# Four 4 KB places for raw weights in place of two of 8 KB, and loads and splits in pieces of at most 1024 elements

## The chip, the cores and the metric

The kernel runs on one core of a Trainium2 chip. The metric is device time in microseconds (us) for one execution; lower is better. The core's engines are TensorE (PE, with its weight loads as PEld), VectorE (DVE), ScalarE (ACT), GpSimd (POOL) and SyncE (SP). SP computes nothing here: it issues nearly all transfers, in the order of its queue.

## The reference

Two transformer blocks over 512 tokens of width 1024, in float32.

```python
def first_block(x, ...):
    h = rmsnorm(x, norm_mix)
    proj = h @ w_in                       # queries, keys, values, gates of two attentions
    y_a = swa_sink_attention(qa, ka, va)  # 8 heads, window 128
    k_cmp = compress(kc, cmp_w1_k, ...)   # gelu(blocks @ w1) @ w2; v_cmp the same
    y_b = nsa_attention(qb, k_cmp, v_cmp, ksl, vsl, kw, vw, gates)
    merged = sigmoid(g_a) * (y_a @ w_up_a) + sigmoid(g_b) * (y_b @ w_up_b)
    x = x + merged @ w_out
    ug = causal_dwconv(rmsnorm(x, norm_ffn) @ w_ffn_in, conv_w, conv_b)
    u, g = split(ug)                      # 2816 each
    x = x + (silu(g) * u) @ w_ffn_out
    return rmsnorm(x, norm_final)

def second_block(x, mem, ...):            # MLA, differential and memory attention
    proj = rms_norm(x) @ w_in_2
    y = concatenate([y_mla, y_diff, y_mem]) * silu(z)
    return x + y @ w_out_2
```

## The kernel before

Every product of activations and weights is done as three matmuls on rounded halves (`mm3`, lines 302 to 309): each operand is H (its value rounded to the matmul type) plus L (the rest), and the three are wH·xH, wH·xL and wL·xH.

So each block of weights goes through three steps. `wload` (line 125) has SP load it from HBM into a tile `raw`. `wsplit` (line 135) writes `wH` on ACT (line 139) and `wL = raw - wH` on DVE or POOL (line 140); each of wH and wL has three buffers of 4 KB of a partition. Then PE reads both. All raw tiles share one tag with two buffers ("places"), each as large as the largest tile: 8 KB of a partition, or 2048 float32 elements. A load can be issued only when the earlier tile in its place has been read for the last time, by the subtraction of line 140.

`dense_steps` (line 314) goes over output columns in tiles of 128. It loads a chunk of 256 columns (8 blocks of 128 rows, so 2048 elements, 1 MB) at a time and splits one tile of 128 columns (1024 elements) per step; a tile is 24 matmuls of 512 columns. Where only 128 columns are wanted (the keys, the compress inputs), the load has 1024 elements, and takes one of the two places all the same. With one group of rows, the next tile's split (and, at a new chunk, its load) is called two k before the end of a tile (`WA`). `ffn` uses it for `w_ffn_in` (a chunk for u, then one for g, 11 column tiles in each of two halves `hf`; the eleventh tile is alone, 128 wide) and for `w_ffn_out` (two groups of 6 and 5 row blocks, 1536 and 1280 elements). `up` has a chunk of 512 with four row blocks. `nat_steps` (line 1124) is the product with tokens on the partitions. `values` loads 4 x 416 elements, and `compress` 8 x 256 of `w1`, used in two halves. `fetch` (line 221) brings weights of the second block, split ahead of time (`presplit`) and stored as H and L, back: three of five into wH and wL, two of five as one tile of 8 KB in the tag `raw`.

The stages follow one another in one program: the norm; the products for the window attention; then `pipeline` over its 8 heads, with `fill1` woven in (memory keys, keys, `compress`, and the queries `qg` of the second attention); then the second attention with `fill2` (the gate product `ga` and `up`); `gb`, `up`, `w_out`; the FFN; and the second block. A scheduler of the framework lays out the program: for each engine it sets one order from the order of the code and its own estimates, and each engine then runs its queue strictly in that order. An instruction that waits holds all that is queued behind it on its engine. The waits for buffers are put in by the framework.

Of the kernel before, what the change touches and what calls it, by code (L numbers as in the profile page):

```python
# [85 lines left out]
class Build:  # L86
# [36 lines left out]


    def wload(self, src, ktn, w):
        raw = self.wp.tile([128, ktn, w], F32, tag="raw", name="raw", bufs=2)
        if isinstance(src, (list, tuple)):
            n = 128 // len(src)
            for i, s in enumerate(src):
                self.nc.sync.dma_start(raw[i * n:(i + 1) * n], s)  # L130
        else:
            self.nc.sync.dma_start(raw, src)
        return raw

    def wsplit(self, raw):
        ktn, w = raw.shape[1], raw.shape[2]
        H = self.wp.tile([128, ktn, w], F32R, tag="wH", name="wH", bufs=3)
        L = self.wp.tile([128, ktn, w], F32R, tag="wL", name="wL", bufs=3)
        self.nc.scalar.activation(H, raw, AF.Copy)  # L139
        self.leng.tensor_sub(L, raw, f32(H))  # L140
        return H, L
# [79 lines left out]
    def fetch(self, key):  # L221

        dst, n, w = self.held.pop(key)
        self.turn = getattr(self, "turn", -1) + 1
        if self.turn % 5 < 3:
            T = [self.wp.tile([128, n * w], F32R, tag=t, name=t, bufs=3) for t in ("wH", "wL")]
            for i in range(2):
                self.nc.sync.dma_start(f32(T[i]), f32(dst[:, i]))
        else:
            t = self.wp.tile([128, 2, n * w], F32R, tag="raw", name="wHL", bufs=2)  # L230
            self.nc.sync.dma_start(f32(t), f32(dst))
            T = [t[:, i] for i in range(2)]
        return [t.rearrange("p (k c) -> p k c", k=n) for t in T]

# [79 lines left out]
    def dense_steps(self, src, groups, c0, cw, xH, xL, evac, chunk=256, tag="mm", mt=128, pre=None):  # L314
# [5 lines left out]
        def weights(i, gi):  # L320
            if pre is not None:
                return next(pre)
            c, o = tiles[i]
            w = min(chunk, c0 + cw - c)
            if o == 0 and gi == 0:
                raws[c] = [self.wload(src(k0, k1, c, w), k1 - k0, w) for k0, k1 in groups]
            return self.wsplit(raws[c][gi][:, :, o:o + min(mt, w - o)])
        k_last = groups[-1][1] - 1
# [177 lines left out]
    def block1(self):  # L506
# [45 lines left out]
        def values():  # L552
            pv = [self.psum(t) for t in ("O", "O", "mm", "mm")]
            for kk in range(0, 8, 4):
                raw = self.wp.tile([128, 4, 416], F32, tag="raw", name="raw", bufs=2)
                for o, c0, w in ((0, 640, 128), (128, 1664, 128), (256, 1920, 160)):
                    nc.sync.dma_start(raw[:, :, o:o + w], W(kk, kk + 4, c0, w))
                for k2 in range(0, 4, 2):
                    H, L = self.wsplit(raw[:, k2:k2 + 2])
                    for b in range(4):  # L560
                        tb = slice(128 * b, 128 * b + 128)
                        for i in range(2):
                            k = kk + k2 + i
                            self.mm3(pv[b][:, :408], hH[:, k, tb], hL[:, k, tb], H[:, i, :408], L[:, i, :408],
                                     k == 0, k == 7)
            for b in range(4):
                self.split(pv[b][:, :384].rearrange("p (h d) -> p h d", d=64), V2[:, b, :, :64], V2[:, b, :, 64:])
                nc.scalar.activation(gate[:, b], pv[b][:, 384:408], AF.Tanh, scale=0.5)
            nc.vector.tensor_scalar(gate, gate, 0.5, 0.5, op0=ALU.mult, op1=ALU.add)
# [166 lines left out]
        QB = []  # L736
        qg = self.dense_steps(W, K8, 768, 512, HH, HL, qevac(QB))

        def fill1():
# [28 lines left out]
            def compress(i):  # L768
# [5 lines left out]
                for k0 in (0, 4, 8, 12, None):  # L774
                    if k0 is not None:
                        if k0 % 8 == 0:
                            raw = self.wload(w1[:, k0:k0 + 8], 8, 256)
                        le = self.leng
                        self.leng = nc.gpsimd if CE >> (k0 // 4) & 1 else nc.vector
                        parts.append((k0, *self.wsplit(raw[:, k0 % 8:k0 % 8 + 4])))  # L780
                        self.leng = le
# [189 lines left out]
        def up(W, y, evac):  # L971
            W = W.rearrange("(g k p) c -> g p k c", g=2, p=64)
            return self.dense_steps(lambda k0, k1, c, w: [W[g][:, k0:k1, c:c + w] for g in range(2)], [(0, 4)], 0, D,
                                    [y[k][:, 0] for k in range(4)], [y[k][:, 1] for k in range(4)], evac, chunk=512)

# [148 lines left out]
    def nat_steps(self, src, ktn, cols, xH, xL, evac, nb=4, tags=("mm", "S"), t=0, tail=False, kf=0, pre=None):  # L1124


        for i, pieces in enumerate(cols):
# [12 lines left out]
            held = []  # L1140
            kr = ktn - kf if pre is not None or (ktn - kf) * w <= 2048 else (ktn - kf) // 2
            step = min(kr, max(1, 1024 // w))
            for k0 in [b + i for b in range(kf, ktn, kr) for i in range(0, kr, step)]:
                k1 = min(ktn, k0 + step)
                if pre is None and (k0 - kf) % kr == 0:
                    raw = self.wp.tile([128, kr, w], F32, tag="raw", name="raw", bufs=2)
                    o = 0
# [826 lines left out]
```

## Time before, and its profile

| | |
|---|---|
| Median of 3 runs | 1069.96 us (1069.77 to 1073.72) |
| The profiled execution's own time | 1068.34 us |
| Its span | 1066.4 us |
| Granted TensorE clock over the span | 0.996 |
| Instructions | 15435 |
| HBM read / written | 128.83 MB / 39.08 MB |

The span reaches from the first to the last instruction of the profiled execution; the rest of that execution's time lies around it. In rows of a timeline the first column is the start in us, the second the duration in us (from the first start to the last end where several are merged), then engine and line, and in brackets how long the engine sat idle before it and what ended that. A matmul's recorded duration overlaps with the next one's, so its rate is read from starts or counts.

### The profile page before, as it was taken

What the parts mean: (1) busy time and instruction counts of PE and PEld (TensorE: products, weight loads), DVE (VectorE), ACT (ScalarE), POOL (GpSimd) and SP (SyncE); (2) the same over time, 40 slices, a digit from 0 to 9 for tenths busy, and PEclk for the clock granted to TensorE, in tenths of its full rate; (3) what the DMA queues carried; (4) which work ended last, traced back from release to release, by engine and by line L of the source; (5) the groups of instructions that cost most, each with busy time, mean ns of one, the idle gap of its engine ahead of it and who ended that gap; (6) DMA issues with size and microseconds to landing.
All of it is one profiled execution on the core that took longest, in us unless ns stands there. A gap on an engine that the chain in (4) does not pass through costs nothing.

```text
span 1066.4 us, 15435 instructions
## 1 busy us (share of the span) xinstructions
PE 1027.0 (96%) x5425; PEld 866.1 (81%) x5425; DVE 751.1 (70%) x1603; ACT 581.3 (55%) x1127; POOL 230.7 (22%) x361
## 2 busy tenths in 40 slices
PE   5999898989999999999999999999999999999898
PEld 4897777878878888888888888887889997887798
DVE  6669884487882375678985478988633497989982
ACT  6557764577783244345553445555643545977630
POOL 4323124222321048000000200000350128230200
PEclk9999999999999999999999999999999999999999
DMA  6645436221213363255769978868855662266442
GB/s 190 177 110 173 104 85 155 52 45 35 57 49 84 79 180 99 80 157 156 224 207 313 313 242 239 255 218 270 296 192 168 220 216 82 80 198 198 138 159 80
DMA packets 131341, 169.98 MB, mean 159 GB/s; under 512 B 8548, under 2 KB 101450, under 8 KB 130112
## 3 DMA queue, kind: packets, MB, share of 16 engines
q1 hardware_dynamic: 127904, 161.50, 49.0%
q0 software_dynamic: 3360, 7.49, 2.9%
q8 instruction: 43, 0.70, 0.3%
q14 instruction: 34, 0.28, 0.1%
HBM read 128.83 MB, written 39.08 MB: 157 GB/s over the span
## 4 chain that ended last, share of the span: by engine, by line
PE 75%; DVE 13%; ACT 4%; DMA 4%; issue 3%; SPq 0%; POOL 0%; POOLq 0%; ACTq 0%; DVEq 0%
PE ps_mm L304 19%; PE ps_mm L309 19%; PE ps_mm L308 19%; PE ps_S L1366 3%; PE ps_T L498 3%; DMA raw<-in_w_in 2%; DVE wL L140 2%; PE ps_O L1395 1%; PE ps_O L1397 1%; PE ps_S L309 1%; PE ps_S L308 1%; PE ps_S L304 1%; DVE PTL L112 1%; ACT e L489 1%; DVE e L487 1%
## 5 line engine op out<-in xcount | busy, mean ns | idle before, releaser
L139 ACT ACTIVATE wH<-raw 128x1024 fp32r<-128x1024 f32 (+4 forms) x145 | 137.3, 947 | 192.1 <-PE ps_mm L308 148.4
L140 DVE TENSOR_TENSOR wL<-raw,wH 128x1024 fp32r<-128x1024 f32 (+4 forms) x130 | 146.3, 1127 | 90.9 <-ACT wH L139 90.5
L304 PE MATMUL ps_mm<-nH,wH 128*128 128x512 f32 x416 | 162.7, 391 | 0.6 <-DVE qL L118 0.6
L309 PE MATMUL ps_mm<-nH,wL 128*128 128x512 f32 x416 | 162.5, 391 | 0.0
L308 PE MATMUL ps_mm<-nL,wH 128*128 128x512 f32 x416 | 162.5, 391 | 0.0
L489 ACT ACTIVATE e<-e,mn 128x256 f32<-128x256 f32 (+5 forms) x160 | 86.3, 541 | 26.8 <-DVE mn L487 25.5
L304 PE MATMUL ps_mm<-hH,wH 128*128 128x512 f32 x232 | 93.6, 404 | 0.0
L309 PE MATMUL ps_mm<-hH,wL 128*128 128x512 f32 x232 | 91.7, 395 | 0.0
L304 PEld LDWEIGHTS ps_mm<-nH,wH 128*128 128x128 f32 x416 | 78.2, 188 | 16.5 <-DVE qL L118 0.8
L308 PE MATMUL ps_mm<-hL,wH 128*128 128x512 f32 x232 | 91.3, 393 | 0.0
L309 PEld LDWEIGHTS ps_mm<-nH,wL 128*128 128x128 f32 x416 | 78.1, 188 | 15.8
L308 PEld LDWEIGHTS ps_mm<-nL,wH 128*128 128x128 f32 x416 | 78.2, 188 | 15.5
L111 ACT ACTIVATE PTH<-ps_T 128x512 fp32r<-128x512 f32 (+1 forms) x108 | 55.6, 528 | 31.6 <-PE ps_T L498 30.9
L112 DVE TENSOR_TENSOR PTL<-ps_T,PTH 128x512 fp32r<-128x512 f32 (+1 forms) x108 | 63.7, 606 | 10.6 <-ACT PTH L111 9.5
L304 PE MATMUL ps_mm<-aH,wH 128*128 128x512 f32 x176 | 68.5, 390 | 1.6 <-ACT aH L111 1.5
L308 PE MATMUL ps_mm<-aL,wH 128*128 128x512 f32 x176 | 68.5, 389 | 0.0
L309 PE MATMUL ps_mm<-aH,wL 128*128 128x512 f32 x176 | 68.5, 389 | 0.0
L498 PE MATMUL ps_T<-ident,e 128*128 128x128 f32 x368 | 62.6, 277 | 6.1 <-DVE e L1739 3.6
L498 PEld LDWEIGHTS ps_T<-ident,e 128*128 128x128 f32 x368 | 44.7, 141 | 22.2 <-DVE e L1739 4.4
L1080 POOL MEMSET cv<- 128x2 f32 x44 | 4.3, 100 | 235.5 <-DVE cc L1084 229.1
L309 PEld LDWEIGHTS ps_mm<-hH,wL 128*128 128x128 f32 x232 | 43.8, 189 | 9.0 <-DVE wL L140 0.2
L304 PEld LDWEIGHTS ps_mm<-hH,wH 128*128 128x128 f32 x232 | 43.8, 189 | 7.2 <-ACT wH L139 0.8
(584 smaller groups left out, 2596.5 us busy)
## 6 DMA issues: line engine op xcount, KB each, us to landing
raw<-in_w_ffn_in SPq DMA_DIRECT2D x20, 1024.0 KB, 5.8
raw<-in_w_in SPq DMA_DIRECT2D x12, 1024.0 KB, 7.6
pre<-in_w_in SPq DMA_DIRECT2D x17, 512.0 KB, 5.6
raw<-in_w_ffn_out SPq DMA_DIRECT2D x8, 768.0 KB, 5.7
raw<-in_w_ffn_out SPq DMA_DIRECT2D x8, 640.0 KB, 6.2
xt<-in_x SPq DMA_DIRECT2D x8, 512.0 KB, 5.0
raw<-in_w_out SPq DMA_DIRECT2D x4, 1024.0 KB, 5.3
pre_z<-preH SPq DMA_DIRECT2D x16, 256.0 KB, 5.1
```

Source lines behind the costliest of these rows:

```text
L111: nc.scalar.activation(H, src, AF.Copy)
L112: nc.vector.tensor_sub(L, src, f32(H))
L139: self.nc.scalar.activation(H, raw, AF.Copy)
L140: self.leng.tensor_sub(L, raw, f32(H))
L304: ins = mm(ps, wH, xH, start=first, stop=False)
L308: mm(ps, wH, xL, start=False, stop=False)
L309: mm(ps, wL, xH, start=False, stop=last)
L487: nc.vector.tensor_tensor_reduce(e, ps, bias, op0=ALU.add, op1=ALU.min, scale=1.0, scalar=3e38, accum_out=mn)
L489: nc.scalar.activation(e, e, AF.Exp, scale=-1.0, bias=mn, accum_out=sm)
L498: nc.tensor.transpose(ps[:, 128 * i:128 * i + 128], blk, self.ident)
L1366: nc.tensor.matmul(ps[:, :n], q[:, 128 * b:128 * b + 128], k[:, :n], start=i == 0, stop=i == len(prods) - 1)
L1395: mm(out, v2(kb), H[:, c], start=first, stop=False)
```

## The change

Raw tiles now hold at most 1024 elements of a partition (4 KB), and there are four of them. `wload` cuts a load along the row blocks into equal pieces of at most 1024 elements, a transfer and a place for each; `wsplit` takes one or several pieces and writes each part of `wH` and `wL` with an instruction of its own. The H and L of a fetched 8 KB tile become two tiles of 4 KB with a transfer each. `qg` loads chunks of 128 columns in place of 256, `up` chunks of 256 in place of 512, `compress` and `values` load per split, and `nat_steps` loads at most 1024 elements at a time.

```diff
+    def rawtile(self, *shape):
+        return self.wp.tile([128, *shape], F32, tag="raw", name="raw", bufs=4)
+
     def wload(self, src, ktn, w):
-        raw = self.wp.tile([128, ktn, w], F32, tag="raw", name="raw", bufs=2)
...
+        n = -(-ktn * w // 1024)
+        step = -(-ktn // n)
+        out = []
+        for k0 in range(0, ktn, step):
+            k1 = min(ktn, k0 + step)
+            raw = self.rawtile(k1 - k0, w)
+            v = src(k0, k1)
...
+                self.nc.sync.dma_start(raw, v)
+            out.append((k0, raw))
+        return out
+
+    def wsplit(self, *pieces):
...
-        self.nc.scalar.activation(H, raw, AF.Copy)
-        self.leng.tensor_sub(L, raw, f32(H))
+        k = 0
+        for p in pieces:
+            c = slice(k, k + p.shape[1])
+            k += p.shape[1]
+            self.nc.scalar.activation(H[:, c], p, AF.Copy)
+            self.leng.tensor_sub(L[:, c], p, f32(H[:, c]))
         return H, L
...
-            t = self.wp.tile([128, 2, n * w], F32R, tag="raw", name="wHL", bufs=2)
-            self.nc.sync.dma_start(f32(t), f32(dst))
-            T = [t[:, i] for i in range(2)]
+            T = [self.wp.tile([128, n * w], F32R, tag="raw", name="wHL", bufs=4) for _ in range(2)]
+            for i in range(2):
+                self.nc.sync.dma_start(f32(T[i]), f32(dst[:, i]))
...
-                raws[c] = [self.wload(src(k0, k1, c, w), k1 - k0, w) for k0, k1 in groups]
-            return self.wsplit(raws[c][gi][:, :, o:o + min(mt, w - o)])
+                raws[c] = [self.wload(lambda a, b: src(k0 + a, k0 + b, c, w), k1 - k0, w) for k0, k1 in groups]
+            return self.wsplit(*(r[:, :, o:o + min(mt, w - o)] for _, r in raws[c][gi]))
...
-            for kk in range(0, 8, 4):
-                raw = self.wp.tile([128, 4, 416], F32, tag="raw", name="raw", bufs=2)
+            for kk in range(0, 8, 2):
+                raw = self.rawtile(2, 416)
...
-        qg = self.dense_steps(W, K8, 768, 512, HH, HL, qevac(QB))
+        qg = self.dense_steps(W, K8, 768, 512, HH, HL, qevac(QB), chunk=128)
...
-                        if k0 % 8 == 0:
-                            raw = self.wload(w1[:, k0:k0 + 8], 8, 256)
+                        raw = self.rawtile(4, 256)
+                        nc.sync.dma_start(raw, w1[:, k0:k0 + 4])
...
-                                    [y[k][:, 0] for k in range(4)], [y[k][:, 1] for k in range(4)], evac, chunk=512)
+                                    [y[k][:, 0] for k in range(4)], [y[k][:, 1] for k in range(4)], evac)
...
-            kr = ktn - kf if pre is not None or (ktn - kf) * w <= 2048 else (ktn - kf) // 2
+            kr = ktn - kf if pre is not None or (ktn - kf) * w <= 1024 else (ktn - kf) // 2
```

## Rows read from the trace of the kernel before

**Rows 1.** The page: busy time and share of each engine; the chain by engine.
```profile
PE 1027.0 (96%) x5425; PEld 866.1 (81%) x5425; DVE 751.1 (70%) x1603; ACT 581.3 (55%) x1127; POOL 230.7 (22%) x361
...
PE 75%; DVE 13%; ACT 4%; DMA 4%; issue 3%; SPq 0%; POOL 0%; POOLq 0%; ACTq 0%; DVEq 0%
```

**Rows 2.** Timeline of PE: starts that followed idle time, with their releasers.
```profile
127.92 0.39 PE L699 MATMUL ps_O<-PTH,V 128*128 128x256 f32 x1 [2.11 <-ACT PTH L111]
...
149.64 0.38 PE L699 MATMUL ps_O<-PTH,V 128*128 128x256 f32 x1 [0.82 <-ACT PTH L111]
150.37 0.39 PE L700 MATMUL ps_O<-PTL,V 128*128 128x256 f32 x1 [0.34 <-DVE PTL L112]
...
171.85 1.14 PE L834 MATMUL ps_T<-w2v,hv 128*128 128x64 f32 x8 [2.31 <-POOL hv L827]
...
741.86 0.50 PE L304 MATMUL ps_mm<-aH,wH 128*128 128x512 f32 x1 [1.47 <-ACT aH L111]
```

**Rows 3.** Timeline of ACT: splits of raw tiles that waited for a transfer.
```profile
125.94 1.06 ACT L139 ACTIVATE wH<-raw 128x1024 fp32r<-128x1024 f32 x1 [2.15 <-DMA raw<-in_w_in]
...
146.73 1.06 ACT L139 ACTIVATE wH<-raw 128x1024 fp32r<-128x1024 f32 x1 [3.46 <-DMA raw<-in_w_in]
...
168.08 1.06 ACT L139 ACTIVATE wH<-raw 128x1024 fp32r<-128x1024 f32 x1 [5.04 <-DMA raw<-in_w_in]
...
723.63 0.85 ACT L139 ACTIVATE wH<-raw 128x768 fp32r<-128x768 f32 x1 [2.46 <-DMA raw<-in_w_ffn_out]
```

**Rows 4.** The chain in order of time, 100 to 176 us: start, us, what.
```profile
107.88 1.14 DVE wL L140
...
116.52 1.20 DVE wL L140
...
117.73 8.13 DMA raw<-in_w_in
...
127.03 1.23 DVE wL L140
...
136.94 1.73 DVE wL L140
...
138.72 7.90 DMA raw<-in_w_in
...
156.58 1.24 DVE wL L140
...
157.83 10.16 DMA raw<-in_w_in
```

**Rows 5.** Windows: us, busy of each engine, clock, DMA share, GB/s.
```profile
100.00:150.00 50.00, 44.59 (x252) 36.15 (x250) 44.15 (x98) 34.49 (x72) 14.39 (x12) 1.00 0.41 95
...
550.00:600.00 50.00, 49.89 (x221) 40.98 (x220) 29.29 (x42) 19.70 (x31) 0.20 (x2) 1.00 0.90 301
...
700.00:750.00 50.00, 48.53 (x215) 39.71 (x214) 42.24 (x62) 28.73 (x44) 0.40 (x4) 1.00 0.75 243
```

**Rows 6.** Timeline of DVE in the FFN, a half block, a weight split, the next.
```profile
712.52 0.68 DVE L207 TENSOR_TENSOR preL<-pre,preH 128x512 fp32r<-128x512 f32 x1
713.12 1.22 DVE L140 TENSOR_TENSOR wL<-raw,wH 128x1024 fp32r<-128x1024 f32 x1
714.25 0.74 DVE L1083 SCALAR_TENSOR_TENSOR cc<-cv,vec_norm_ffn,cc 128x512 f32<-128x512 f32 x1
```

**Rows 7.** Timeline of SP: the first loads of `w_ffn_out` in the second half.
```profile
716.32 3.08 SPq L132 DMA_DIRECT2D raw<-in_w_ffn_out x2
```

**Rows 8.** The tile `raw`: instructions by line, ns min/median/max, forms.
```profile
L139 ACT ACTIVATE wH<-raw x145: 613/1058/1075, 12.6 to 783.7; 128x1024 fp32r<-128x1024 f32 x93, 128x512 fp32r<-128x512 f32 x16, 128x768 fp32r<-128x768 f32 x16, 128x640 fp32r<-128x640 f32 x16
L140 DVE TENSOR_TENSOR wL<-raw,wH x130: 683/1221/1983, 23.6 to 784.5; 128x1024 fp32r<-128x1024 f32 x86, 128x768 fp32r<-128x768 f32 x16, 128x640 fp32r<-128x640 f32 x16, 128x512 fp32r<-128x512 f32 x8
```

**Rows 9.** DMA issues: count, KB each, median us from issue to landing.
```profile
raw<-in_w_ffn_in SPq DMA_DIRECT2D x20, 1024.0 KB, 5.8
...
raw<-in_w_ffn_in SPq DMA_DIRECT2D x4, 512.0 KB, 4.9
```

More of the change, by code (lines that the diff above doesn't have):

```diff
@@ L122, in show @@
             self.nc.sync.dma_start(self.dbg[name], ap)
+    def rawtile(self, *shape):
+        return self.wp.tile([128, *shape], F32, tag="raw", name="raw", bufs=4)
     def wload(self, src, ktn, w):
-        raw = self.wp.tile([128, ktn, w], F32, tag="raw", name="raw", bufs=2)
[L127 to L136, printed above, removed]
+        n = -(-ktn * w // 1024)
[5 more added lines that the diff above has]
+            v = src(k0, k1)
+            if isinstance(v, (list, tuple)):
+                m = 128 // len(v)
+                for i, t in enumerate(v):
+                    self.nc.sync.dma_start(raw[i * m:(i + 1) * m], t)
+            else:
+                self.nc.sync.dma_start(raw, v)
+            out.append((k0, raw))
+        return out
+    def wsplit(self, *pieces):
+        w = pieces[0].shape[2]
+        ktn = sum(p.shape[1] for p in pieces)
         H = self.wp.tile([128, ktn, w], F32R, tag="wH", name="wH", bufs=3)
         L = self.wp.tile([128, ktn, w], F32R, tag="wL", name="wL", bufs=3)
-        self.nc.scalar.activation(H, raw, AF.Copy)
-        self.leng.tensor_sub(L, raw, f32(H))
+        k = 0
[4 more added lines that the diff above has]
+            self.leng.tensor_sub(L[:, c], p, f32(H[:, c]))
         return H, L
@@ L553, in values @@
             pv = [self.psum(t) for t in ("O", "O", "mm", "mm")]
-            for kk in range(0, 8, 4):
-                raw = self.wp.tile([128, 4, 416], F32, tag="raw", name="raw", bufs=2)
+            for kk in range(0, 8, 2):
+                raw = self.rawtile(2, 416)
                 for o, c0, w in ((0, 640, 128), (128, 1664, 128), (256, 1920, 160)):
[L557 to L565, printed above, removed]
+                    nc.sync.dma_start(raw[:, :, o:o + w], W(kk, kk + 2, c0, w))
+                H, L = self.wsplit(raw)
+                for b in range(4):
+                    tb = slice(128 * b, 128 * b + 128)
+                    for i in range(2):
+                        k = kk + i
+                        self.mm3(pv[b][:, :408], hH[:, k, tb], hL[:, k, tb], H[:, i, :408], L[:, i, :408],
+                                 k == 0, k == 7)
             for b in range(4):
@@ L775, in compress @@
                     if k0 is not None:
-                        if k0 % 8 == 0:
-                            raw = self.wload(w1[:, k0:k0 + 8], 8, 256)
+                        raw = self.rawtile(4, 256)
+                        nc.sync.dma_start(raw, w1[:, k0:k0 + 4])
                         le = self.leng
                         self.leng = nc.gpsimd if CE >> (k0 // 4) & 1 else nc.vector
-                        parts.append((k0, *self.wsplit(raw[:, k0 % 8:k0 % 8 + 4])))
+                        parts.append((k0, *self.wsplit(raw)))
                         self.leng = le
@@ L1145, in nat_steps @@
                 if pre is None and (k0 - kf) % kr == 0:
-                    raw = self.wp.tile([128, kr, w], F32, tag="raw", name="raw", bufs=2)
+                    raw = self.rawtile(kr, w)
                     o = 0
```

## The prediction

> **What bounds the kernel now.** I read the page first: PE is busy for 1027.0 of 1066.4 us and 75% of the chain that ended last is PE's [rows 1]. So only what leaves PE idle (39.4 us in all) or makes the idle time longer can move the end; a faster load that no one waits for is worth nothing. Next, the windows: in the FFN PE never pauses (221 matmuls in 49.89 us, so 0.226 us each, at full clock) although DMA is at its most loaded there, 0.90 of its time, while the window attention with its woven products keeps PE at 44.59 of 50 us [rows 5]. Then I went through PE's timeline for every start behind idle time. Some lie ahead of the first product and touch no raw weight; many short ones belong to the softmax work. Five are left that I trace back to a weight split: 2.11, 0.82, 0.34, 2.31 and 1.47 us [rows 2], 7.05 in all. That is nearly the whole of what the change can win.
>
> How a load stops PE although PE waits for no weight: ACT runs its queue in order, and four splits on it sat 2.15, 3.46, 5.04 and 2.46 us for a transfer [rows 3]. Behind the first stands PTH, for which PE then waited until 127.92; behind the second the PTH of 149.64, and its L part on DVE. Behind the third, DVE's subtraction is late, behind it on DVE the copy `hid`, POOL's `hv` after that, and PE starts again at 171.85 [rows 2].
>
> And why the transfers are late: the chain shows each as issued when a place comes free and not before. A subtraction starts at 116.52 and takes 1.20 us; the load is issued at 117.73. One starts at 136.94 and takes 1.73; the next load goes at 138.72. One starts at 156.58 and takes 1.24; the third goes at 157.83 [rows 4]. They then need 8.13, 7.90 and 10.16 us to land. In this stretch a 512 KB tile of keys holds an 8 KB place, so two loads are all that can be on their way or in use.
>
> **The change part by part.**
>
> *Four places in the window attention.* Write down the order of loads there: second compress weight quarter w1k1, w1k2, w1k3, the v input (1408), q0, q1, w1v0, w1v1, q2, w1v2, w1v3, q3, then the two pieces of the gate chunk ga. Each now takes one place of four, so a load waits for the split of the item four before it.
> - q0 waits for w1k1, whose subtraction begins at 107.88 and takes 1.14 [rows 4]: issue from 109.02 in place of 117.73, 8.71 us sooner. ACT came to that split 2.15 us before 125.94 [rows 3], at 123.79; even at 8.13 us the load lands by 117.2. The wait and the 2.11 us of PE go.
> - q2 waits for q0, whose subtraction ends at 127.03 + 1.23 = 128.26 [rows 4]: 10.46 us sooner than 138.72. At 7.90 it lands at 136.2, and ACT came at 146.73 - 3.46 = 143.27 [rows 3]. The 0.82 and 0.34 us go.
> - ga's first piece waits for q2, which was split at 146.73 [rows 3], so it goes some 8 us sooner than 157.83; its second waits for w1v2, split somewhere between there and 157.82 [rows 4], and may still hold ACT. Of the 2.31 us I count 1.6 as gained, between 0 and all.
> That is 2.11 + 0.82 + 0.34 + 1.6 = 4.9 us. Who is late next is DVE: it is busy for 44.15 of 50 us there [rows 5], so up to half of this may come back as waits for DVE: 2.4 to 5.6 us (with the 2.31 whole).
>
> *The end of the FFN's second half.* The eleventh column tile of u and of g is a 512 KB load each, and the two fill both places, so the loads of `w_ffn_out` go at 716.32 and after [rows 7], right behind the subtraction that starts at 713.12 [rows 6] and SP's stores. The split waits 2.46 us [rows 3], DVE loses time behind it, and PE waits 1.47 us at 741.86 for aH [rows 2]. With four places the two single tiles take two and the first two pieces of `w_ffn_out` the others, which come free with the chunk before, a tile of 24 matmuls (24 x 0.226 = 5.4 us) sooner. The wait of 2.46 goes. I take 1.0 of the 1.47, as DVE stays full (42.24 of 50 [rows 5]); bounds 0 and 1.47.
>
> *More instructions.* Of the 93 splits with 1024 elements [rows 8], 68 become two by the code (window queries 4, ga 8, gb 8, `w_out` 8, `w_ffn_in` 40); all 32 with 768 or 640 do too. So 100 more activations and 100 more subtractions. On a full DVE the step from start to start is 713.12 - 712.52 = 0.60 us for 512 elements and 714.25 - 713.12 = 1.13 for 1024 [rows 6]: two halves cost 1.20, so 0.07 more each, 7 us over the kernel if all were on DVE (93 - 86 = 7 splits of that size have it on POOL [rows 8]). By recorded durations the upper bound is 2 x 0.683 - 1.221 = 0.145 on DVE and 2 x 0.613 - 1.058 = 0.168 on ACT [rows 8], 15 and 17 us. None of it is in the stretch of 112 to 172, where every split keeps its size. In the FFN it lies beside 5.4 us of matmuls per tile with DVE at 84% [rows 5]; at 0.07 to 0.15 per tile the cover holds. What would be late without the cover is aH and aL at the end of a half: some four doubled subtractions stand there, 0.3 us, which I count as lost. Against it, the first half of a split can feed matmuls before the second is done; PE in the FFN has no pause that this could fill, so nothing.
>
> *More transfers.* A chunk of 1 MB becomes two loads of 512 KB; packets stay as long in HBM (1 KB rows) but for qg (512 B). By the rows, 512 KB of `w_ffn_in` land in 4.9 us and 1 MB in 5.8 [rows 9]. A chunk lasts PE 2 x 5.4 = 10.8 us, so even two loads one after the other (9.8) fit. Cost nothing; the other end of the bound is a rival below. The Trainium skill speaks against smaller loads: "DMA: Bandwidth & Descriptors", Rules for kernel authors, wants at least 1 MiB per DMA, and its fit under "Anatomy of one DMA" is 2.0 us plus the bytes over 436 GB/s; by that fit, an estimate, two halves in a row take 6.4 us where one whole takes 4.4. The trace is slower than the fit but has the same shape, and either result is below what a chunk lasts PE, so by the page too the sum stays.
>
> *The fetched weights, `up`, `values`, `compress`, `nat_steps`.* The same bytes are held and the same number of tiles is in use; H and L take a place each. SP issues more, which only matters where SP is late, and PE shows no wait on a transfer there. Nothing, within 1 us either way, as the scheduler will lay out all queues anew.
>
> **Sum.** -4.9 - 1.0 + 0.3 = -5.6 us against the profiled execution's 1068.34: 1062.7. The median stands 1.62 us above that execution, so 1064.4, or 0.52% less than 1069.96.
>
> **The rivals.**
> - *DVE takes over.* The transfers come early, but DVE, already at 44.15 of 50 [rows 5], sets the pace in the stretch, so that half of the 4.9 and none of the 1.0 is won and the 0.3 lost: -2.15, or 1067.8. For it: DVE is 13% of the chain [rows 1]. Against: while ACT waited, DVE waited too.
> - *The loads don't come earlier.* The places are there, but SP's order puts each load just ahead of its split, and all ACT waits stay: 1070, the time of before with at most the 0.3. Against it: three times out of three the load left within 0.05 us of the subtraction that freed its place [rows 4], so SP stood ready.
> - *Slower: halves land one after the other.* If in the FFN each 512 KB piece took as long as 1 MB now (5.8 us [rows 9]), a chunk would need 11.6 us against 10.8, and each of 20 two-tile chunks would add 0.8 us: 16 us, with the rest as forecast about 1080. It decides from 5.4 us a piece. For it: DMA at 0.90 [rows 5]. Against: the bytes and packets of the FFN stay the same, and pieces can overlap.
> - *More than counted.* All 7.05 us go, and with them some 3 of PE's other idle time (39.4 in all), as splits off ACT's and DVE's way let the softmax work come sooner: 1060.
>
> **How the numbers follow.** Forecast (1061 to 1066.5) 0.45; DVE takes over 0.20; loads no earlier 0.12; slower 0.08; more 0.15. The predicted time is 1064.4. The range 1058 to 1070.5 leaves out the slower case and a little at either end. Half a percent, 5.35 us, is about what a measurement of this kernel tells from no change; below 1064.6 it is faster. Of the forecast's span of 5.5 us, 3.6 lie below that, two thirds, which makes 0.29; with the last case 0.44 faster. The slower case is 0.08, and the rest, 0.48, no change.
>
> **What would show it.** Right: ACT's splits in the window attention no longer wait for DMA, and PE's pauses of 2.11, 0.82 and 2.31 are gone; the stretch up to the gate product is 4 to 5 us shorter; the pause before the first aH product of `w_ffn_out` shrinks; in the FFN PE stays at 221 or 222 matmuls per 50 us. Wrong: loads still leave behind the subtraction two before; new waits of PE for DVE in 112 to 172; in the FFN, splits that wait for transfers with PE pausing; or a new order of the queues that opens pauses far from the weights.

## The result, and the profile after

The changed kernel takes 1058.75 us (median of 4 runs, 1058.01 to 1060.0), against 1070.1 for the kernel before beside it (1069.77 to 1073.72): a ratio of 0.9879, 95% interval 0.986 to 0.9898. That is 11.35 us less, where 5.6 were forecast. The direction was right and most of the places were, and the time lies in the range, but the size is out by a factor of two. The profiled execution has a span of 1056.3 us and took 1058.04.

The page after, its lines on busy time and on the chain by engine [rows 1]:

```profile
PE 1022.2 (97%) x5425; PEld 863.8 (82%) x5425; DVE 759.5 (72%) x1697; ACT 591.1 (56%) x1227; POOL 226.1 (21%) x367
...
PE 79%; DVE 13%; ACT 4%; issue 2%; DMA 1%; POOLq 0%; POOL 0%; SPq 0%; ACTq 0%; DVEq 0%
```

The span lost 10.1 us. PE's idle time fell only from 39.4 to 34.1 us; the other 4.8 came out of its *busy* time, with the same 5425 matmuls. Half of the gain was never idle time in the records, so a sum of pauses could not have found it. At a lower clock a matmul is busy for longer, as below, and behind a pause one is recorded as longer too: the two with PTH in [rows 2] take 0.39 and 0.38 us, most of that form with no pause ahead 0.28. What else lies in the 4.8 us stays open.

Where it went: windows that end at the same matmul in both kernels. First the kernel before, from 95 us on (us, then busy time and count of PE, PEld, DVE, ACT and POOL; PE's granted clock; DMA share; GB/s):

```profile
95.00:125.40 30.40, 28.73 (x165) 23.38 (x164) 27.91 (x59) 22.02 (x47) 8.64 (x12) 1.00 0.48 113
125.40:148.20 22.80, 19.89 (x117) 16.61 (x116) 19.65 (x49) 14.33 (x29) 4.49 (x2) 1.00 0.33 73
148.20:172.80 24.60, 20.04 (x105) 15.41 (x103) 17.51 (x30) 15.06 (x28) 5.02 (x8) 1.00 0.48 122
172.80:213.00 40.20, 40.20 (x202) 33.76 (x202) 15.55 (x47) 21.09 (x46) 17.08 (x14) 1.00 0.37 89
213.00:226.30 13.30, 11.10 (x55) 9.34 (x54) 12.17 (x33) 7.14 (x18) 3.43 (x3) 0.87 0.35 79
```

And the changed kernel in the same five stretches, then in the three of [rows 5]:

```profile
95.60:124.60 29.00, 27.88 (x165) 23.11 (x164) 27.38 (x60) 24.54 (x51) 8.56 (x12) 1.00 0.53 128
124.60:145.30 20.70, 20.07 (x118) 16.91 (x118) 19.67 (x50) 14.70 (x34) 6.71 (x3) 1.00 0.32 88
145.30:165.50 20.20, 18.66 (x105) 15.45 (x103) 16.63 (x30) 13.02 (x24) 5.06 (x9) 1.00 0.60 155
165.50:205.70 40.20, 40.20 (x202) 33.72 (x202) 14.79 (x46) 20.72 (x49) 15.91 (x18) 1.00 0.27 63
205.70:217.50 11.80, 9.85 (x55) 7.81 (x54) 11.59 (x33) 6.67 (x17) 3.57 (x4) 1.00 0.44 90
...
100.00:150.00 50.00, 48.17 (x280) 40.09 (x279) 47.07 (x109) 40.25 (x83) 15.05 (x12) 1.00 0.47 115
550.00:600.00 50.00, 49.72 (x219) 40.62 (x218) 26.63 (x48) 20.43 (x40) 3.16 (x10) 1.00 0.92 290
700.00:750.00 50.00, 49.88 (x220) 40.93 (x220) 41.39 (x65) 29.09 (x52) 4.41 (x6) 1.00 0.77 255
```

Stretch by stretch the change is worth -1.4, -2.1, -4.4, 0 and -1.5 us. The third is the one to look at: 105 matmuls in both, PE idle 4.56 before and 1.54 after (-3.0), and their busy time down by 1.4 as well, at a full clock in both. A further 1.3 us went behind these stretches, nearly all at the end of the FFN, and the first 95 us cost 0.6; together that is the 10.1. The first and the last of the five stretches, 2.9 us, are in no term of the sum. The FFN's steady part is as it was: the window has 219 matmuls, at a DMA share of 0.92, where 221 or 222 were forecast, but matmul for matmul (the k-th of one kernel against the k-th of the other) nothing moves: from the 2750th to the 3400th both take 147.3 us.

The loads leave sooner, as forecast. SP issues those for q0, q2 and the gate product's first piece at these times (starts, changed kernel), against 117.73, 138.72 and 157.83 before [rows 4]; 8.71, 10.46 and some 8 us were forecast, 9.8, 17.0 and 13.9 came (up to 3 us of it is the kernel's own lead by then):

```profile
107.93 0.38 SPq L143 DMA_DIRECT2D raw<-in_w_in  x1
...
121.69 0.37 SPq L143 DMA_DIRECT2D raw<-in_w_in  x1
...
143.93 0.37 SPq L143 DMA_DIRECT2D raw<-in_w_in  x1
```

They also land sooner (median us from issue to landing, kernel before, then the changed one):

```profile
raw<-in_w_in SPq DMA_DIRECT2D x12, 1024.0 KB, 7.6
...
raw<-in_w_in SPq DMA_DIRECT2D x29, 512.0 KB, 4.6
```

Why the middle is shorter is seen on ACT. Its waits for raw weights by source (us in all, times, longest), kernel before:

```profile
ACT wH L139 <- DMA raw<-in_w_ffn_out: 12.7, 5, 3.9
ACT wH L139 <- DMA raw<-in_w_in: 10.6, 3, 5.0
ACT wH L139 <- DMA raw<-in_w_ffn_in: 3.4, 1, 3.4
```

The changed kernel:

```profile
ACT wH L157 <- DMA raw<-in_w_ffn_out: 15.9, 6, 3.6
ACT wH L157 <- DMA raw<-in_w_ffn_in: 8.1, 5, 3.8
ACT wH L157 <- DMA raw<-in_w_mem_kv: 2.1, 1, 2.1
```

The three waits for `in_w_in` [rows 3] are gone. In the FFN ACT now waits longer than before, and PE hardly notices: it has one new pause there, of 0.28 us at 551.25, for an aH at the end of the first half. PE's pauses of 0.25 us or more between 110 and 172 us are now these (timeline, starts behind idle time); none goes back to a transfer, the largest is DVE's:

```profile
112.04 0.39 PE L716 MATMUL ps_O<-PTH,V 128*128 128x256 f32 x1 [0.58 <-ACT PTH L111]
117.39 0.51 PE L322 MATMUL ps_mm<-hH,wH 128*128 128x512 f32 x1 [0.27 <-ACT wH L157]
133.11 0.30 PE L825 MATMUL ps_T<-ident,gx 62*128 62x62 f32 x2 [0.58 <-DVE gx L821]
...
157.69 0.39 PE L717 MATMUL ps_O<-PTL,V 128*128 128x256 f32 x1 [1.24 <-DVE PTL L112]
```

Ahead of that PTL in DVE's queue stands a weight subtraction that is recorded as 1.77 us beside two GpSimd instructions; one of the same size takes 0.67 at 154.00:

```profile
154.94 1.77 DVE L158 TENSOR_TENSOR wL<-raw,wH 128x512 fp32r<-128x512 f32 x1
```

### The profile page after: what moved, and what is told of

It is laid out like the page before. It is cut to its first block, busy times and chain, and to the rows that moved or that the text cites. A ratio compares the mean times of both kernels' runs of the same rounds, so it can differ in the third digit from the quotient of the medians.

```text
span 1056.3 us, 15851 instructions
## 1 busy us (share of the span) xinstructions
PE 1022.2 (97%) x5425; PEld 863.8 (82%) x5425; DVE 759.5 (72%) x1697; ACT 591.1 (56%) x1227; POOL 226.1 (21%) x367
## 4 chain that ended last, share of the span: by engine, by line
PE 79%; DVE 13%; ACT 4%; issue 2%; DMA 1%; POOLq 0%; POOL 0%; SPq 0%; ACTq 0%; DVEq 0%
PE ps_mm L322 20%; PE ps_mm L327 20%; PE ps_mm L326 20%; PE ps_S L1383 3%; PE ps_T L516 2%; DVE wL L158 2%; DVE e L505 1%; DVE PTL L112 1%; PE ps_O L1414 1%; PE ps_O L1412 1%; PE ps_S L327 1%; PE ps_S L326 1%; PE ps_S L322 1%; ACT e L507 1%; DMA xt<-in_x 1%
## 5 line engine op out<-in xcount | busy, mean ns | idle before, releaser
L157 ACT ACTIVATE wH<-raw 128x512 fp32r<-128x512 f32 (+4 forms) x245 | 150.0, 638 | 196.4 <-PE ps_mm L326 134.6
L158 DVE TENSOR_TENSOR wL<-raw,wH 128x512 fp32r<-128x512 f32 (+3 forms) x224 | 161.9, 741 | 85.9 <-ACT wH L157 82.9
L505 DVE CUSTOM_DVE_ANT_0 e<-ps_S,G 128x128 f32<-128x128 f32 (+1 forms) x64 | 30.7, 485 | 27.3 <-PE ps_S L1383 27.1
```

The lines of the kernel that those rows point to most:

```text
L157: self.nc.scalar.activation(H[:, c], p, AF.Copy)
L158: self.leng.tensor_sub(L[:, c], p, f32(H[:, c]))
L505: nc.vector.tensor_tensor_reduce(e, ps, bias, op0=ALU.add, op1=ALU.min, scale=1.0, scalar=3e38, accum_out=mn)
```

## The experiments

The theory after this reading had three parts: (a) splits in the window attention and at the end of the FFN no longer hold ACT for a transfer; (b) GpSimd's queue has one long subtraction in a better place, so that VectorE isn't held up beside it; (c) with fewer pauses PE's clock falls less often. The rivals were that pieces alone, or places alone, hold the gain. Each run stands against runs of the kernel before on the same chip (medians 1070.6 to 1071.8), so ratios compare best; that of the changed kernel is 0.9879.

**Pieces without places.** The kernel before, its two places of 8 KB loaded and split in pieces of at most 1024 elements. The chunks stay as they were, so the queries' loads still bring 256 columns:

```diff
-            self.nc.sync.dma_start(raw, src)
...
+            for k0 in range(0, ktn, step):
+                k1 = min(ktn, k0 + step)
+                self.nc.sync.dma_start(raw[:, k0:k1], src[:, k0:k1])
...
+            c = slice(k0, min(ktn, k0 + step))
+            self.nc.scalar.activation(H[:, c], raw[:, c], AF.Copy)
+            self.leng.tensor_sub(L[:, c], raw[:, c], f32(H[:, c]))
```

> The kernel before with loads and splits cut into the same pieces of at most 1024 elements, but the two places of 8 KB kept. Theory (places): the gain is that a small load no longer blocks 8 KB, so here the window attention keeps its pauses; ACT's splits wait for transfers of w_in again, some 10 us in all, and the time is 1068 to 1072. Rival (pieces): shorter instructions and loads feed PE sooner, so most of the gain is here too, 1058 to 1063.

Measured 1067.52, ratio 0.9959 (0.9938 to 0.9979), just under the theory's range. But that is a gain and a loss. By 205 us it is 3.9 us ahead of the kernel before, matmul for matmul; at the ends of the two halves of the FFN it loses 3.8 and 2.1. PE waits there (its timeline):

```profile
556.54 0.73 PE L312 MATMUL ps_mm<-aH,wH 128*128 128x512 f32 x2 [2.13 <-ACT aH L111]
...
740.66 0.50 PE L312 MATMUL ps_mm<-aH,wH 128*128 128x512 f32 x1 [2.04 <-ACT aH L111]
```

and windows just behind them show the granted clock at 0.50, half of full speed:

```profile
558.00:561.00 3.00, 3.00 (x8) 2.35 (x8) 2.32 (x4) 1.57 (x3) 0.00 (x0) 0.50 0.87 257
...
742.50:745.50 3.00, 3.00 (x8) 2.30 (x7) 1.02 (x2) 0.23 (x2) 0.00 (x0) 0.50 1.08 378
```

Its splits wait 11.9 us for `in_w_ffn_in`, against 3.4 before and 8.1 in the changed kernel. So halves with only two places lose in the FFN, where the same halves with four places don't; that the late splits ahead of aH are the cause is argued from these waits. This kernel also lacks the gain at 104 us that is told below under GpSimd: its lead does not change there.

**Places filled as before.** The changed kernel, with the window attention's loads filling two places each (512-element pieces for the keys and the compression's inputs, queries 256 columns at once, the compression's weights 8 blocks at a time; two of its edits):

```
-qg = self.dense_steps(W, K8, 768, 512, HH, HL, qevac(QB), chunk=128)
+qg = self.dense_steps(W, K8, 768, 512, HH, HL, qevac(QB))
...
-yield from self.dense_steps(W, K8, 1280, 128, HH, HL, cevac(0))
+yield from self.dense_steps(W, K8, 1280, 128, HH, HL, cevac(0), most=512)
```

> The changed kernel with the four places filled as the two were in the window attention's products: each load of 128 key or compress columns takes two places (as two pieces of 512 elements), qg has chunks of 256 again (two pieces, used by two tiles), compress loads 8 x 256 at once in two pieces. All else as changed. Theory: 7 to 9 of the 10 us come back, 1065 to 1068, with ACT's splits waiting for transfers of w_in again. Rival: the gain is spread over the kernel; 1060 to 1063.

Measured 1066.06, ratio 0.9941 (0.9917 to 0.9964): 7.3 us of the 11.35 are back by the medians, 6.6 by the ratios, as the theory has it. Not all of it is places, though: in this trace the gain at 104 us is gone as well (between the 500th and the 545th matmul it wins 0.05 us on the kernel before, the changed kernel 1.86), so the run undoes two things at once.

**The queries' loads alone**, once in the changed kernel (back to 256 columns) and once in the kernel before (to 128 columns, two places of 8 KB as they are):

```
-qg = self.dense_steps(W, K8, 768, 512, HH, HL, qevac(QB), chunk=128)    # changed kernel
+qg = self.dense_steps(W, K8, 768, 512, HH, HL, qevac(QB))
-qg = self.dense_steps(W, K8, 768, 512, HH, HL, qevac(QB))               # kernel before
+qg = self.dense_steps(W, K8, 768, 512, HH, HL, qevac(QB), chunk=128)
```

> The changed kernel, but the second group of queries is again loaded 256 columns at a time, which fills two places at once, instead of 128 columns and one place. Theory (the splits that PE waited for at 127.92, 149.64 and 150.37 are those of these queries, and a piece of its own for each 128 columns is what brings them forward): most of what filling the places as before gave back (7.3 us) comes back by this alone, 1062.5 to 1065. Rival (what counts are the keys', values' and compression's loads ahead in the same queue): 1058.5 to 1061.

> The kernel before with one argument changed: the second group of queries is loaded 128 columns (1024 elements of a partition) at a time, each into a place of 8 KB, of which there are still two. Theory (what PE waited for at 127.92, 149.64, 150.37 and 171.85 were the loads of these queries and of what follows them, and a load of half the size is there sooner also with two places): 3 to 4.5 us less in the window attention, and nothing in the feed-forward, 1066 to 1068. Rival (it is the number of places that counts; half-filled places bring loads no sooner): 1069.5 to 1071.5.

Measured 1063.41, ratio 0.9926 (0.991 to 0.9942), and 1066.83, ratio 0.9949 (0.9931 to 0.9968). Both theories hold. The one argument is worth 0.51% with two places and 0.9926 - 0.9879 = 0.47% with four; the rest of the change is worth 0.74% without it and 0.70% with it. The parts add up, though each ratio is known to some 0.2% only. By the times some 40% of the gain is an argument that needed no new places. The traces show a third, all of it in the window attention: up to 173 us the argument wins 3.5 us with two places, and taking it back loses 3.1 with four. Beyond that lie a wait for fetched weights (1.9 us, at 789 in the kernel with 256 columns) and, with two places, a low clock from 170.8 on that costs 1.6. The argument does not do all of what four places do. The kernel before with it has this left of ACT's waits for `in_w_in`, and PE still pauses where `hv` is late:

```profile
ACT wH L139 <- DMA raw<-in_w_in: 5.7, 2, 5.0
...
168.95 0.32 PE L834 MATMUL ps_T<-w2v,hv 128*128 128x64 f32 x1 [2.28 <-POOL hv L827]
```

Its first query load leaves no sooner than before (118.37), but lands 4.9 us after its issue in place of 8.13.

**The end of the FFN.** The eleventh tile of u and of g in each half is loaded as two 512-element pieces, so that each of these tiles fills two places (the edit for u; that for g is the same):

```
-                             lambda m, ps: us.append(conv(ps, i0 + i + m))), pre, 8, at)
+                             lambda m, ps: us.append(conv(ps, i0 + i + m)),
+                             most=512 * n), pre, 8, at)
```

> The changed kernel, but the eleventh tile of each half of the feed-forward (the single one) is loaded in two pieces of 512 elements that fill two places each, as before the change a single tile filled a whole place of two. Theory (a place that comes free late at the end of the second half made the pause of 1.47 us at 741.86 in the kernel before): a pause of PE comes back near 731, and the time goes up by 0.5 to 1.5 us, to 1059.3 to 1060.3. Rival (the pause went for another cause, such as the down-projection's loads in pieces): no pause there, 1058.75 within 0.5 us.

Measured 1061.69, ratio 0.9915 (0.9898 to 0.9933): slower by more than the theory's range. The pause is back where it was forecast (timeline of PE):

```profile
551.90 0.73 PE L322 MATMUL ps_mm<-aH,wH 128*128 128x512 f32 x2 [0.81 <-ACT aH L111]
...
733.62 0.50 PE L322 MATMUL ps_mm<-aH,wH 128*128 128x512 f32 x1 [1.27 <-ACT aH L111]
```

The first is 0.28 in the changed kernel and the second isn't there: matmul for matmul 1.64 us at the two ends together. Another 1.34 us lie at 787, where PE waits for fetched weights; the runs with the whole gate subtraction (1.40) and with the 256 columns (1.9) show the same wait without any edit near it, so I don't count it to the tile.

**GpSimd beside VectorE.** In the stretch from 95 us a subtraction of POOL and a scaling of DVE meet. Kernel before, timelines of both:

```profile
103.68 2.60 DVE L682 TENSOR_SCALAR e<-e,sm 128x130 f32<-128x130 f32 x1
...
103.28 0.73 POOL L652 DMA_DIRECT2D ast<-rvec  x1 [0.82 <-POOL qy L632]
104.03 2.16 POOL L762 TENSOR_TENSOR X<-X,X 128x992 fp32r<-128x992 f32 x1
```

The scaling ends at 106.28, 0.09 us behind the subtraction. The changed kernel has the subtraction ahead of the DMA issue in POOL's queue:

```profile
101.55 1.28 POOL L649 TENSOR_TENSOR qy<-yt,qy 64x512 fp32r<-64x512 f32 x1 [3.51 <-ACT qy L648]
102.79 2.14 POOL L779 TENSOR_TENSOR X<-X,X 128x992 fp32r<-128x992 f32 x1
104.88 0.73 POOL L669 DMA_DIRECT2D ast<-rvec  x1
```

It is over at 104.93, and the first scaling takes 0.75 us:

```profile
104.27 0.75 DVE L699 TENSOR_SCALAR e<-e,sm 128x130 f32<-128x130 f32 x1
```

Between the 500th and the 545th matmul, on either side of this, the changed kernel gains 1.86 us. The Trainium skill has the rule in "SBUF — State Buffer", under "SBUF: two separate sides": VectorE and GpSimd share a port pair that one of them holds for a whole instruction while the other is blocked; for VectorE that goes for instructions with two inputs in SBUF or in a mode that uses two ports, and whichever starts first gets the pair. The trace agrees on the blocking (the end 0.09 us behind). By the recorded starts it does not agree on who wins, as the scaling of the kernel before starts first, at 103.68 against 104.03, with a DMA issue of GpSimd just ahead. A copy ahead of the subtraction brings the long scaling back:

```
-nc.gpsimd.tensor_sub(x2[:, :, 1, :62], xv, f32(x2[:, :, 0, :62]))
+nc.gpsimd.tensor_copy(x2[:, :10, 1, :62], f32(x2[:, :10, 0, :62])); nc.gpsimd.tensor_sub(x2[:, :, 1, :62], xv, f32(x2[:, :, 0, :62]))
```

> The changed kernel with the compression's X subtraction on GpSimd put off by a copy of 620 elements of a partition ahead of it (some 1 us), so that it runs beside VectorE's scaling again, as it did before the change. Theory (the 1.86 us that the changed kernel won between 105 and 112 us came from the order of GpSimd's queue and nothing else, and no later wait gives it back): VectorE's scaling there takes 1.5 to 2.6 us instead of 0.75, PE loses 1.0 to 1.9 us, and the time is 1059.8 to 1060.7. Rival (a later wait of PE would have taken the time anyway): a pause there, and 1058.75 within 0.5 us at the end.

```profile
102.54 0.69 POOL L779 CAST X<-X 128x620 fp32r<-128x620 f32 x1
103.31 2.14 POOL L779 TENSOR_TENSOR X<-X,X 128x992 fp32r<-128x992 f32 x1
```

The subtraction runs until 105.45, the first scaling takes 1.52 us, and the gain between the same two matmuls is 1.09 in place of 1.86. No later wait swallows it: 50 us on, the kernel is 1.3 us behind the changed one. The median is 1061.9, ratio 0.9906 (0.9886 to 0.9927), more than the theory's 1059.8 to 1060.7; the profiled execution also has the wait for fetched weights and a low clock from 986 to 990, neither near the edit. So the traces show the sign and 0.8 to 1.3 us of the size; the times agree in sign, with intervals that still overlap, and the rest is not shown.

**Three groups of subtractions moved to DVE**, in the kernel before and in the changed one (the X of above, the output's yL, and the first key weights):

```
-                    nc.gpsimd.tensor_sub(x2[:, :, 1, :62], xv, f32(x2[:, :, 0, :62]))
+                    nc.vector.tensor_sub(x2[:, :, 1, :62], xv, f32(x2[:, :, 0, :62]))
-                (nc.gpsimd if YP >> m & 1 else v).tensor_sub(yL[m], y32[m], f32(yH[m]))
+                v.tensor_sub(yL[m], y32[m], f32(yH[m]))
-        self.leng = nc.gpsimd
+        self.leng = nc.vector
```

> The kernel before, with three groups of subtractions moved from GpSimd to VectorE, the same arithmetic: the compression's X (2.16 us on GpSimd at 104.03, beside which VectorE's scaling took 2.60 us), the low halves yL of the second block's output (four at 987.83, 5.94 us, beside which four VectorE instructions took 5.00 us), and the low half of the first key weights (2.59 us at 13.71, beside which x's scaling took 2.58 us). Theory (a GpSimd subtraction holds up a VectorE instruction that reads and writes SBUF until it ends, and in the kernel before this fell on the path at 104 us, in the changed kernel not, because GpSimd's queue has the subtraction one place sooner): 1.0 to 1.9 us less between 100 and 112, 1.5 to 2.5 less between 985 and 1000, 0.3 to 1.0 less in the first 20 us; 1066 to 1068. Rival (VectorE pays with its own time for what it takes over, some 6 us): 1070 to 1072.

> The changed kernel with the same three groups of subtractions on VectorE. Theory: the part at 104 us is already gone by the order of GpSimd's queue, so only the other two are won, 2 to 3.5 us: 1055.3 to 1056.8, and the difference to the kernel before with the same edit is 1 to 2 us smaller than that between the changed kernel and the kernel before. Rival (GpSimd's order at 104 us gave the change nothing): the two differences are equal within 0.5 us. Second rival: VectorE pays for it, 1058.5 to 1060.

Measured 1065.78, ratio 0.9951 (0.9933 to 0.997), and 1055.0, ratio 0.9847 (0.983 to 0.9865): both better than forecast by a few tenths. With the edit the two kernels differ by 10.8 us in place of 11.35 or, by ratios, 1.05% in place of 1.21%: so 0.6 to 1.8 us of the change's gain would belong to POOL's order. That points theory (b)'s way, but it is less than the intervals of the ratios leave open (some 0.2% each), so by these times neither the size nor the sign is shown. Where the first 20 us got shorter (1.0 us in the changed kernel), the lead is gone by 127 us: the next wait takes it. In the second block the changed kernel has

```profile
978.11 4.99 DVE L1756 SCALAR_TENSOR_TENSOR e<-e,sm,e 128x128 f32<-128x128 f32 x4
...
978.31 5.93 POOL L1866 TENSOR_TENSOR yL<-y,yH 128x512 fp32r<-128x512 f32 x4 [6.96 <-ACT yH L1865]
```

and with yL on DVE the same four instructions take 1.94 us, with PE's pauses of 0.80, 0.88 and 0.78 gone.

**The gate's subtraction whole.** In the changed kernel POOL's subtraction ahead of the gate product is in two halves:

```
-yield from self.dense_steps(W, K8, 2072, D, HH, HL, ga)
+yield from self.dense_steps(W, K8, 2072, D, HH, HL, ga, chunk=128)
```

> The changed kernel, but the gate product ga loads chunks of 128 columns, so that each of its splits is one piece of 1024 again, and POOL's subtraction is one instruction of 2.4 us instead of two of 1.3. Theory: of the 1.5 us won between 213 and 226 us of the kernel before, most is that a DVE instruction no longer waits out a POOL instruction of 2.4 us, and that PE's pause there no longer brings the clock down for 3.4 us; so 0.5 to 1.7 us come back, 1059.3 to 1060.5, and a DVE scaling of about 2.4 us beside POOL's subtraction is in the trace. Rival: the stretch won by the order of the queues or by transfers; no change, 1058.3 to 1059.2.

Measured 1059.83, ratio 0.9887 (0.9868 to 0.9906): inside the theory's range, but not to be told from the changed kernel's 0.9879, so the size is read from the trace. DVE, POOL and PE there:

```profile
207.92 2.36 DVE L1436 TENSOR_SCALAR e<-e,sm 128x128 f32<-128x128 f32 x1
...
207.83 2.38 POOL L158 TENSOR_TENSOR wL<-raw,wH 128x1024 fp32r<-128x1024 f32 x1 [11.64 <-ACT wH L157]
...
211.38 0.63 PE L943 MATMUL ps_T<-ident,pc 128*128 128x128 f32 x4 [2.16 <-DVE pc L938]
```

The changed kernel has 0.85 us for that scaling and a pause of 1.74: the halves are worth 0.42. But the stretch gained 1.5, and of that 1.1 is there with the whole subtraction too; it is the clock. The kernel before pauses 2.20 us at the same matmul and is then granted 0.50, the lower level of 1.2 GHz (windows, 2 us each):

```profile
218.00:220.00 2.00, 1.11 (x5) 1.14 (x6) 2.00 (x7) 0.00 (x0) 0.00 (x0) 0.71 0.22 49
220.00:222.00 2.00, 2.00 (x6) 1.71 (x6) 1.59 (x6) 1.98 (x6) 0.53 (x1) 0.50 0.98 247
```

The kernel with the whole subtraction, after a pause of 2.16:

```profile
210.00:212.00 2.00, 0.62 (x5) 0.65 (x6) 2.00 (x6) 0.00 (x0) 0.21 (x1) 1.00 0.10 27
212.00:214.00 2.00, 2.00 (x11) 1.60 (x10) 2.00 (x8) 1.96 (x6) 0.53 (x1) 1.00 0.88 230
```

So much the same pause is followed by the lower level in one execution and not in the other, and a single profile of each kernel can't tell whether the change has a part in that.

**x ahead of the raw loads.** The changed kernel, with three of the four places held until x's last block has landed, because x lands later at the start:

```
+held = [self.rawtile(1, 8) for _ in range(3)]
...
+if i:
+    for h in held:
+        nc.vector.tensor_tensor(h[:, 0], h[:, 0], xt[:, 3, :8], op=ALU.add)
```

> The changed kernel with three of the four places held at the start until the last block of x has landed, so that only the first load of weights runs beside x. Theory: the changed kernel starts its products 1.16 us later than the kernel before, half of it because x's last block lands 0.56 us later beside one more load, half because DVE splits a piece ahead of the activations' L; here x lands at 9.2 us or sooner and the first product starts 0.5 to 1.5 us sooner than in the changed kernel: 1057.3 to 1058.2. Rival: the order of DVE's queue alone sets it, and the later weights make the first split late: 1058.7 to 1060.

Measured 1059.32, ratio 0.9876 (0.9857 to 0.9895): no gain, as the rival has it. ACT shows why; the held load is now late for a split that stands ahead of the norm's `hH` in ACT's queue:

```profile
15.20 0.63 ACT L157 ACTIVATE wH<-raw 128x512 fp32r<-128x512 f32 x1 [1.05 <-DMA raw<-in_w_in]
```

**The rest of the first block's GpSimd subtractions.** On top of the three groups, first the gate's and up-projection's weights on DVE (`POOLL = 14` to `12`), then the attention outputs too (`OE = 1` to `0`):

> The changed kernel with the three groups of subtractions on VectorE, and with the low halves of the gate's and the up-projection's weights on VectorE too (in the changed kernel 19 subtractions of 1.29 us on GpSimd between 166 and 290 us). Theory (a GpSimd subtraction stretches VectorE's scaling beside it: 0.85 and 1.26 us for two instructions that take 0.34 and 0.16 elsewhere, ahead of PE's pause of 1.74 us at 211.15): that pause shrinks to under 0.5 us, and the time falls by 0.8 to 1.6 us below that of the three groups alone (1055.0): 1053.4 to 1054.2. Rival (VectorE takes over some 13 us of work in a stretch where it works 70 to 80% of the time, and its waits return as pauses of PE): 1055 to 1058.

> As the kernel with all these subtractions on VectorE, and the 16 subtractions of the attention outputs (qy, 23.8 us on GpSimd, each stretched to 1.75 to 2.23 us where VectorE's weight subtractions run beside it) on VectorE as well, so that GpSimd has hardly a long instruction left in the first block. Theory (each pair on both engines takes as long as the two one after the other, so moving one of them costs VectorE nothing): same as without this edit, within 1 us. Rival (VectorE becomes the bound of the window attention, where it works over 90% of most stretches): 3 to 8 us slower.

Measured 1052.45 (1052.28 to 1053.93), ratio 0.982 (0.9799 to 0.9841), and 1058.34, ratio 0.9871 (0.9851 to 0.9891). The first goes the theory's way, by 1 us more than its range: the scaling takes 0.19 us, the pause of 1.74 is gone, and this is the best version, 6.3 us below the changed kernel. The second is the rival's: in the window attention PE waits for DVE by 1.56 and 1.15 us at 120.52 and 126.19, so there DVE has no room left: the kernel is 5.9 us slower than without the last edit.

## Why the prediction fell short

*What bounds the kernel.* PE, as said. The step that failed is the ceiling set there: "Five are left that I trace back to a weight split: ... 7.05 in all. That is nearly the whole of what the change can win." It rests on the premise that "only what leaves PE idle (39.4 us in all) or makes the idle time longer can move the end", and 4.8 of the 10.1 us came out of PE's busy time. Those five pauses went, but they were not the whole. In the profiled pair the places forecast gave 7.8 us, 2.9 came in stretches without a term, and 0.6 was lost at the start. A ceiling made of recorded pauses left out three things, below. The list was not complete either: two starts that waited for a split itself, 0.35 us at 154.00 and 0.20 at 155.87 in the kernel before, are not in it, and they went too.

*Four places in the window attention.* The mechanism is as told: loads that leave 9.8 to 17 us sooner, splits that no longer wait, and the pauses of 2.11, 0.82, 0.34 and 2.31 [rows 2] gone. The term was mis-sized at 4.9; the stretches from 125 to 173 us gave 2.1 + 4.4 = 6.5. q0's 2.11 came true (2.1). For the rest 2.76 were counted and 4.4 measured, 1.4 of them in matmuls recorded as busy. And the cause was split in the wrong place: I gave it all to the four places, where the 128-column loads of the queries take away the pauses of 2.11, 0.82 and 0.34 with two places as well (a new one of 1.22, at 151.75, is there instead). The 2.31 needed more than that.

*The end of the FFN.* Taken at 1.0 of 1.47; 1.37 went, measured between the same matmuls, and undoing that part alone brought 1.64 back over both halves. The term was right, and the caution in it not needed.

*More instructions, more transfers, fetched weights.* Counted as +0.3, 0 and 0 ± 1. DVE is busy 8.4 and ACT 9.8 us more, for 100 activations and 100 subtractions, as counted. (The prediction has the packets as long as before but for the queries' loads; by the code `up`'s rows halve too.) What PE shows of it in the FFN is 0.36 us at the end of the first half, close to the 0.3. The loads of `w_ffn_in` are now 44 of 512 KB and land in a median of 4.8 us (1 MB took 5.8 [rows 9]). The Trainium skill's advice against loads under 1 MiB ("DMA: Bandwidth & Descriptors", Rules for kernel authors) did no harm to set aside here with four places: the smaller loads of the queries carry a third or more of the gain. The fit that the prediction took from that page is given there for transfers issued from GpSimd; these loads are SP's, and what counts is the trace's 4.8 and 5.8 us. At the start there is a cost: 1.16 us at the first product of the keys, where a second weight split stands ahead of the norm's L parts on DVE and x's first product starts 0.56 later. The sum had nothing there. That it costs little in the end is argued, not shown: a lead of that size was gone by 127 us when the three groups' edit gave it.

*What no term held.* First, POOL's order at 104 us: 1.86 in the trace, of which putting the subtraction off by a copy took back 0.8 to 1.3. "A new order of the queues" stood in the prediction only as a danger; it was a gain. Second, the gate's subtraction in halves: 0.42. Third, the clock. Over 35 executions of the kernel before in these runs the mean granted clock is 0.9952 and the mean span 1069.6 us; four of the changed kernel have 0.9988 and 1057.15. A line through the 35 gives 0.61 us of span for each 0.001, so 3.6 thousandths are 2.2 us. The three of the 35 at full clock have spans of 1065.8 to 1067.0, and the two of the changed kernel 1056.3 and 1057.7: 9.4 us apart. In the profiled pair the kernel before stands at 0.50 from 218.8 to 222.2 us and from 993.7 to 997.1, the changed one nowhere before its last microsecond. Only the 1.1 us at the gate product are set apart by a run, the one with the whole subtraction, which has the pause without the low clock. The rest of this share is argued, not isolated: pauses and low clock come together.

*The rivals.* "More than counted" (1060, a chance of 0.15) was nearest in time and half right in its reason. "The loads don't come earlier" is refuted by ACT's waits. "DVE takes over" holds only for what is left, the pause of 1.24 at 157.69, and there a subtraction beside GpSimd is part of why DVE is late. "Slower: halves land one after the other" didn't happen. The run with two places lost 5.9 us in the FFN, but at its two ends and not chunk by chunk (from the 2700th to the 3450th matmul its lead stays at 1.77 us), so by another way than that rival's: what mattered was how many places there are to have halves under way.

## What to carry to other kernels

Before buying more buffers, try the smaller load: it is ready sooner, and here one argument brought a third to 40% of the gain. But smaller loads with too few places can lose elsewhere, as the FFN did with two. A sum of recorded pauses is no ceiling for such a gain; compare what the whole stretch takes with what its matmuls take at their steady rate. And look for instructions of VectorE that end together with one of GpSimd: moving 27 subtractions off GpSimd won more than half as much again as the change, while moving 16 more, where VectorE is full, cost nearly all of that.

## What the runs showed of the hardware

A VectorE scaling from SBUF to SBUF can last as long as the GpSimd subtraction beside it: 2.36 for one of 128 elements that takes 0.19 alone, with its end 0.07 to 0.09 us behind the other's in the four cases that I looked at (the kernel before at 106.19, the whole gate subtraction at 210.21, the changed kernel at 104.93, and the copy's at 105.45). It can begin before the subtraction's recorded start and be held all the same (103.68 against 104.03; a DMA issue of GpSimd, 0.73 us long, lies just ahead).

After pauses of 2.20 and 2.16 us at the same matmul, the execution of one kernel was granted 0.50 for the next 3.4 us and that of the other 1.00. At the product with `hv` it is the other way round: the kernel before kept 1.00 behind 2.31 us, and with 128-column queries it went to 0.50 behind 2.28. Single executions of the kernel before range from a mean of 0.990 with a span of 1073.8 to 1.000 with 1065.8. All five timed runs of the best version stand at 1.000. What decides whether a pause is followed by the lower level stays open.
